# Forgetting attention: adding the two halves of a block's accumulator on GpSimd, one half moved between rows by DMA

## The chip, the cores and the metric

The kernel runs on one core of one Trainium2 chip. The metric is the device time of one execution in microseconds (us). Runs of the same kernel differ by about 0.1%: the kernel before took 2542.85 to 2546.45 us in three runs, with a median of 2545.35 us.

The core has five engines with a queue each: TensorE (PE; its weight loads are listed as PEld), VectorE (DVE), ScalarE (ACT), GpSimd (POOL) and SyncE (SP). Here SyncE only issues transfers for the core's 16 DMA engines. An engine takes its instructions in program order, and one that waits for a semaphore holds those behind it.

## The reference

Two layers of a trunk on 2048 tokens of width 1024, all in float32. Each layer normalizes x, projects it by one weight, mixes tokens in three branches (spatial gating, retention, forgetting attention), gates each branch, and projects the result back. The change lies in the third branch, which has six heads of width 64:

```python
def _forgetting_attention(q, k, v, f_logit):
    scale = d ** -0.5
    cum_f = jnp.cumsum(jax.nn.log_sigmoid(f_logit), axis=1)
    for i in range(s // Q_BLOCK):
        logits = jnp.einsum('bqhd,bkhd->bhqk', qb, kb) * scale
        logits = logits + cum_f[:, :, q0:q1, None] - cum_f[:, :, None, :q1]
        logits = jnp.where(causal, logits, -jnp.inf)
        p = jax.nn.softmax(logits, axis=-1)
        outs.append(jnp.einsum('bhqk,bkhd->bqhd', p, vb))

f_out = f_out.reshape(b, s, F_WIDTH) * jax.nn.silu(f_g)
```

## The kernel before

Each layer runs as three stages on TensorE: the input projection with gating and retention, the attention, and the output projection. Every float32 operand of a matmul is split into a high and a low part (`H`/`L`, `PH`/`PL`), so that a product is a sum of fast matmuls.

**The attention stage** (`fox`) goes over heads 0 to 5, over four blocks `s` of 512 queries each, and over the 4s + 4 key tiles `j` of 128 keys that a block sees: 240 steps a layer. One step has five parts in the order `ORDER = "ltesv"`:

- `t_step` transposes four pieces of exponentials into a bank `T` (L661) and makes the parts `PH` and `PL` of it, three steps ahead of their use. Usually ScalarE makes PH (L673) and VectorE PL (L672). For the key tiles in `ON_POOL` (tile 3 of block 0; 5 of block 1; 4 and 8 of block 2; 4, 8 and 12 of block 3) ScalarE copies T to SBUF (L666) and GpSimd makes both (L667, L668).
- `l_step` issues the VectorE half that the step before put off.
- `e_step` takes exponentials on ScalarE (L648).
- `s_step` computes scores for later blocks, about 19 steps ahead (L614 with the keys' high parts, L615 with the tile `kL`), and VectorE takes their running minimum `mn` (L632).
- `v_step` multiplies with the values into the bank `acc` (L690 with PH, L691 with PL). The values are 128 columns wide, the high parts in the first 64 and the low parts in the last 64, so `acc` holds two halves, one in rows 0 to 63 and one in rows 64 to 127, and the attention output is their sum.

**After each block** a generator, `finish(h, s, acc)`, runs beside the loop; each `bg.tick()` at the end of a step takes it to its next `yield`. A pair of heads (even e = 0, odd e = 1) shares a tile `o2`, one in its upper and one in its lower 64 rows.

- First tick: ScalarE copies the lower half of acc to a tile `lo` (L703).
- Second tick: VectorE adds the halves into o2 (L705) and sums the denominators (L710). For an even head that is all.
- For an odd head VectorE takes the reciprocal (L713) and SyncE loads the gate (L716). Two ticks on TensorE transposes the reciprocals (L719), ScalarE copies them (L721), and SyncE writes 4 KB of them to DRAM (L723). Two ticks on SyncE reads them back, broadcast over 64 rows, twice (L726). Four ticks on GpSimd multiplies gate and reciprocals (L728), one tick on it multiplies o2 with that (L730), and three ticks on SyncE writes the result (L732).

**Loads** of the next head's keys, values and queries go through a list in `FoxLoads`; one entry is issued on SyncE in each step (L569), ahead of `bg.tick()`. After the last key tile of block 0, and behind the tick of that step, `ld.kv(h + 1)` puts three loads on the list (two of 512 KB, one of 1024 KB), for heads 1 to 4; after block 1 `ld.c(h + 1)` puts on the two `kL` loads of the next head.

The order of all this is the program's order; nothing rearranges it. Tiles of tag "u" share 29 slots in turn.

Of the kernel before, what the change touches and what calls it, by code (L numbers as in the profile page):

```python
# [10 lines left out]
F32 = mybir.dt.float32  # L11
F32R = mybir.dt.float32r
AF = mybir.ActivationFunctionType
ALU = mybir.AluOpType
# [4 lines left out]
P = 128  # L19
# [4 lines left out]
HD = 64  # L24
# [13 lines left out]
FX, RA, RB, RC, RD = 2, 2, 4, 1, 3  # L38
# [32 lines left out]
def wait(n):  # L71
    for _ in range(n):
        yield
# [3 lines left out]
def trunk(ctx, tc, a, out):  # L77
    nc = tc.nc
# [8 lines left out]
    up = ctx.enter_context(tc.tile_pool(name="up", bufs=NU))  # L87
# [3 lines left out]
    def U(name, dt=F32):  # L91
        return up.tile([P, 1024], dt, name=name, tag="u")
# [3 lines left out]
    def bank(name, tag):  # L96
        n, bufs = BANKS[tag]
        return ps.tile([P, n], F32, name=name, tag=tag, bufs=bufs)
# [4 lines left out]
    def small(name, shape, bufs=4):  # L103
        return tp.tile(shape, F32, name=name, tag=name, bufs=bufs)
# [466 lines left out]
    class Fox:  # L571
# [124 lines left out]
        def finish(self, h, s, acc):  # L696
            m, e = divmod(h, 2)
            if e == 0 and s % 2 == 0:
                self.o2[s // 2] = U("o2")
            o2 = self.o2[s // 2][:, (s % 2) * 512:(s % 2 + 1) * 512]  # L700
            yield
            lo = up.tile([HD, 512], F32, name="lo", tag="u")
            nc.scalar.copy(out=lo, in_=acc[HD:P, :])  # L703
            yield
            nc.vector.tensor_tensor(out=o2[e * HD:(e + 1) * HD], in0=acc[0:HD, :], in1=lo, op=ALU.add)  # L705
            if e == 0:
                self.rd[s] = small("rd", [P, 2, 4], bufs=6)
            rd = self.rd[s]
            den = self.den.pop((h, s))
            nc.vector.tensor_reduce(out=rd[:, e], in_=den[:, :, 0:s // 2 + 1], op=ALU.add, axis=AX.X)  # L710
            if e == 0:
                return
            nc.vector.reciprocal(out=rd, in_=rd)  # L713
            gy = U("gy")
            g, rb = gy[:, 0:512], gy[:, 512:1024]
            nc.sync.dma_start(out=g, in_=self.gscr[m][:, s * 512:(s + 1) * 512])  # L716
            yield from wait(FX)
            T = bank("rT", "S")
            nc.tensor.transpose(T[0:8, 0:P], rd.rearrange("p e r -> p (e r)"), ident)  # L719
            rT = tp.tile([8, P], F32, name="rT", tag="yr")  # L720
            nc.scalar.activation(out=rT, in_=T[0:8, 0:P], func=AF.Copy, scale=0.5)  # L721
            scr = dram.tile([8, P], F32, name=f"rd{self.ld.l}{m}{s}")
            nc.sync.dma_start(out=scr, in_=rT)  # L723
            yield from wait(RA)
            for i in range(2):
                nc.sync.dma_start(out=rb[i * HD:(i + 1) * HD], in_=scr[4 * i:4 * i + 4].rearrange("r p -> (r p)").partition_broadcast(HD))  # L726
            yield from wait(RB)
            nc.gpsimd.tensor_tensor(out=g, in0=g, in1=rb, op=ALU.mult)  # L728
            yield from wait(RC)
            nc.gpsimd.tensor_tensor(out=rb, in0=o2, in1=g, op=ALU.mult)  # L730
            yield from wait(RD)
            nc.sync.dma_start(out=self.y[s][1][m], in_=rb)  # L732
# [203 lines left out]
    for l in range(depth):  # L936
# [3 lines left out]
        for i in fox(fx):  # L940
            if i >= len(fx.V) - OW and i % OD:
                next(og, None)
            if l == depth - 1 and i == len(fx.V) - OPRE:
                op = out_proj(l, y, W, og, x_src, lambda t: out[t * P:(t + 1) * P, :], None, None, None)
            elif i == len(fx.V) - OPRE:
# [5 lines left out]
                op = out_proj(l, y, W, og, x_src, lambda t, x1=x1: x1[t], hT, (nw, W0), cur)  # L951
# [44 lines left out]
```

## Time and profile before

| | |
|---|---|
| median of 3 runs | 2545.35 us (2542.85 to 2546.45) |
| the profiled execution | 2542.31 us, of which the span of its instructions is 2540.5 us |
| PE busy | 2500.7 us (98%) |
| PEld busy | 2139.5 us (84%) |
| DVE busy | 1658.1 us (65%) |
| ACT busy | 1258.9 us (50%) |
| POOL busy | 865.4 us (34%) |
| DMA | 229.87 MB, 90 GB/s on average, nearly all from SP's queue |

The shares are averages over stages with different limits, so the attention stages (about 800 to 1089 and 2060 to 2349 us) are read by themselves. A row of the timeline gives start and duration in us, the engine, the line, the operation, what it writes and reads, and in brackets how long the engine was idle before it and what released it. "SPq" is SyncE issuing a transfer; the duration is that of the issue, not of the transfer.

### The profile page before, as it was taken

How to read it: one execution, taken by the hardware profiler on the slowest of the kernel's cores; microseconds unless marked ns; L12 is line 12 of the kernel's file. 1: busy time of each engine (PE TensorE's matmuls, PEld its weight loads, DVE VectorE, ACT ScalarE, POOL GpSimd, SP SyncE). 2: the span in 40 equal slices, each digit the busy share in tenths (PEclk: the TensorE clock that was granted, in tenths of full speed). 3: DMA queues.
4: the chain of work that ended last, by engine and by line, in shares of the span. 5: the costliest groups of instructions: out<-in, count | busy, mean ns of one | idle time of the engine just before them, and what ended most of it. 6: DMA issues, size and time to landing. Idle time of an engine off the chain costs nothing. (4 is left out here: it accounts for less than half of the span.)

```text
span 2540.5 us, 39565 instructions
## 1 busy us (share of the span) xinstructions
PE 2500.7 (98%) x13112; PEld 2139.5 (84%) x13112; DVE 1658.1 (65%) x4161; ACT 1258.9 (50%) x2967; POOL 865.4 (34%) x1384
## 2 busy tenths in 40 slices
PE   9999999999999999999999999999999999999998
PEld 8988899887888888878898889997878888887887
DVE  5544477667668999854454445676666689998433
ACT  7634433333335888843344444333333368888222
POOL 3111366444433333331120114664444323244200
PEclk9999999999999999999999999999999999999999
DMA  6335411101041445253432354111010414543443
GB/s 210 119 91 123 109 46 34 41 14 42 10 109 42 100 109 149 72 183 132 138 124 75 99 121 112 29 38 42 14 38 19 103 45 108 123 132 102 156 149 116
DMA packets 187061, 229.87 MB, mean 90 GB/s; under 512 B 23272, under 2 KB 128680, under 8 KB 185320
## 3 DMA queue, kind: packets, MB, share of 16 engines
q1 hardware_dynamic: 186856, 227.34, 31.9%
q8 instruction: 104, 1.70, 0.3%
q14 instruction: 101, 0.83, 0.1%
HBM read 149.20 MB, written 78.09 MB: 89 GB/s over the span
## 5 line engine op out<-in xcount | busy, mean ns | idle before, releaser
L491 PE MATMUL z<-HL 128*128 128x512 f32 (+2 forms) x1536 | 587.4, 382 | 2.4 <-ACT HL L176 2.4
L493 PE MATMUL z<-HL 128*128 128x512 f32 (+2 forms) x1536 | 561.3, 365 | 0.6 <-DVE HL L178 0.4
L492 PE MATMUL z<-HL 128*128 128x512 f32 (+2 forms) x1536 | 560.0, 365 | 1.5 <-POOL HL L178 1.5
L178 DVE TENSOR_TENSOR HL<-hT,HL 128x512 fp32r<-128x512 f32 x576 | 426.1, 789 | 41.7 <-ACT HL L176 33.2
L869 PE MATMUL oo<-HL 128*128 128x512 f32 x1488 | 355.4, 395 | 0.3 <-DVE HL L178 0.2
L178 POOL TENSOR_TENSOR HL<-wf,HL 128x384 fp32r<-128x384 f32 (+2 forms) x162 | 190.7, 1183 | 430.9 <-ACT HL L176 326.5
L176 ACT CAST HL<-hT 128x512 fp32r<-128x512 f32 x576 | 323.8, 626 | 0.0
L869 PEld LDWEIGHTS oo<-HL 128*128 128x128 f32 x1488 | 273.3, 188 | 57.9 <-DVE HL L178 1.2
L493 PEld LDWEIGHTS z<-HL 128*128 128x128 f32 x1536 | 288.8, 188 | 33.9 <-DVE HL L178 2.0
L491 PEld LDWEIGHTS z<-HL 128*128 128x128 f32 x1536 | 290.3, 189 | 24.5 <-ACT HL L176 3.3
L492 PEld LDWEIGHTS z<-HL 128*128 128x128 f32 x1536 | 290.3, 189 | 24.1 <-POOL HL L178 1.9
L672 DVE TENSOR_TENSOR PHL<-T,PHL 128x512 fp32r<-128x512 f32 (+3 forms) x402 | 241.3, 604 | 17.5 <-ACT PHL L673 17.4
L673 ACT CAST PHL<-T 128x512 fp32r<-128x512 f32 (+3 forms) x402 | 206.4, 520 | 56.6 <-PE T L661 41.2
L266 PE MATMUL z<-HL 128*128 128x512 f32 x576 | 224.4, 390 | 0.0
L267 PE MATMUL z<-HL 128*128 128x512 f32 x576 | 224.1, 389 | 0.0
L268 PE MATMUL z<-HL 128*128 128x512 f32 x576 | 224.1, 389 | 0.0
L614 PE MATMUL S<-kv,q 128*128 128x512 f32 (+1 forms) x480 | 211.0, 442 | 2.0 <-DVE mn L632 2.0
L350 ACT COPY v<-z 128x128 f32<-128x128 f32 x96 | 25.6, 267 | 354.0 <-DVE w L346 353.9
L690 PE MATMUL acc<-PHL,kv 128*128 128x512 f32 x480 | 181.0, 377 | 0.0
L691 PE MATMUL acc<-PHL,kv 128*128 128x512 f32 x480 | 176.3, 367 | 0.9 <-DVE PHL L672 0.9
L648 ACT ACTIVATE row<-row,mn 128x1024 f32<-128x1024 f32 (+2 forms) x192 | 158.2, 824 | 35.9 <-DVE mn L632 35.9
L615 PE MATMUL S<-kL,q 66*128 66x512 f32 (+1 forms) x480 | 175.9, 366 | 0.0
(160 smaller groups left out, 4348.6 us busy)
## 6 DMA issues: line engine op xcount, KB each, us to landing
x<-x SPq DMA_DIRECT2D x48, 512.0 KB
qk<-zHL SPq DMA_DIRECT2D x192, 128.0 KB
wf<-w_in SPq DMA_DIRECT2D x96, 192.0 KB
vscr<-vv SPq DMA_DIRECT2D x32, 384.0 KB
wf<-w_in SPq DMA_DIRECT2D x48, 256.0 KB
kv<-qk SPq DMA_DIRECT2D x24, 512.0 KB
kv<-vscr SPq DMA_DIRECT2D x12, 1024.0 KB
q<-qk SPq DMA_DIRECT2D x48, 256.0 KB
```

Of the source, the lines that this page charges most:

```text
L176: nc.scalar.copy(out=v(H), in_=src)
L178: eng.tensor_tensor(out=v(L), in0=src, in1=v(H), op=ALU.subtract)
L266: mm(z, lhsT=wH[:, c], rhs=H, start=(k == 0), stop=False)
L267: mm(z, lhsT=wH[:, c], rhs=L, start=False, stop=False)
L268: mm(z, lhsT=wL[:, c], rhs=H, start=False, stop=(k == KT - 1))
L491: mm(z[:, :n], lhsT=H[:, c], rhs=wH[:, :n], start=(k == 0), stop=False)
L492: mm(z[:, :n], lhsT=H[:, c], rhs=wL[:, :n], start=False, stop=False)
L493: mm(z[:, :n], lhsT=L[:, c], rhs=wH[:, :n], start=False, stop=(k == KT - 1))
L614: mm(S[:, :n], lhsT=Q[0][:, qc], rhs=K[:, kc], start=True, stop=False)
L672: self.low = lambda: nc.vector.tensor_tensor(out=PL[:, c0:], in0=T[:, c0:], in1=PH[:, c0:], op=ALU.subtract)
L673: nc.scalar.copy(out=PH[:, c0:], in_=T[:, c0:])
L869: mm(oo[g], lhsT=x[:, c], rhs=w[g][i], start=(k == 0 and first), stop=(k == KT - 1 and last))
```

## The change

ScalarE copies the whole accumulator, 128 rows, to the left half of a tile `two`. A DMA on SyncE's queue copies the 64 rows that belong to the other head of the pair into the rows of this head, in the right half of the tile. GpSimd adds the two halves into o2, two ticks later than VectorE did before: for an even head behind a wait of FX = 2 ticks, for an odd head behind the issue of L723's DMA.

```diff
-            lo = up.tile([HD, 512], F32, name="lo", tag="u")
-            nc.scalar.copy(out=lo, in_=acc[HD:P, :])
+            two = U("two")
+            mine, other = (slice(e * HD, (e + 1) * HD), slice((1 - e) * HD, (2 - e) * HD))
+            nc.scalar.copy(out=two[:, 0:512], in_=acc)
+            nc.sync.dma_start(out=two[mine, 512:1024], in_=two[other, 0:512])
             yield
-            nc.vector.tensor_tensor(out=o2[e * HD:(e + 1) * HD], in0=acc[0:HD, :], in1=lo, op=ALU.add)
             if e == 0:
                 self.rd[s] = small("rd", [P, 2, 4], bufs=6)
             rd = self.rd[s]
             den = self.den.pop((h, s))
             nc.vector.tensor_reduce(out=rd[:, e], in_=den[:, :, 0:s // 2 + 1], op=ALU.add, axis=AX.X)
             if e == 0:
+                yield from wait(FX)
+                nc.gpsimd.tensor_tensor(out=o2[mine], in0=two[mine, 0:512], in1=two[mine, 512:1024], op=ALU.add)
                 return
...
             nc.sync.dma_start(out=scr, in_=rT)
+            nc.gpsimd.tensor_tensor(out=o2[mine], in0=two[mine, 0:512], in1=two[mine, 512:1024], op=ALU.add)
             yield from wait(RA)
```

## Rows read from the trace of the kernel before

**Rows 1.** Busy us of each engine in the first attention stage, granted clock, DMA.
```profile
800.00:1089.00 289.00, 283.54 (x1748) 239.58 (x1747) 262.84 (x715) 251.76 (x550) 106.57 (x116) 1.00 0.42 110
```
**Rows 2.** Waits of TensorE, whole trace: us in total, times, longest.
```profile
PE T L661 <- DVE PHL L672: 7.1, 15, 1.3
...
PE S L614 <- DVE mn L632: 2.0, 9, 0.2
```
**Rows 3.** Groups by line: count, busy us, mean ns, idle before.
```profile
L705 DVE TENSOR_TENSOR o<-acc,lo 64x512 f32<-64x512 f32 x48 | 32.7, 681 | 0.8
...
L728 POOL TENSOR_TENSOR gy<-gy 128x512 f32<-128x512 f32 x24 | 31.0, 1293 | 59.1 <-DMA gy<-rd 40.1 <-ACT PHL L673 7.0 <-DVE mn L632 5.9
```
**Rows 4.** Timeline of ScalarE at the end of block 0, head 1.
```profile
856.54 0.58 ACT L703 COPY lo<-acc 64x512 f32<-64x512 f32 x1
857.15 1.07 ACT L673 CAST PHL<-T 128x512 fp32r<-128x512 f32 x2
```
**Rows 5.** Timeline of SyncE, GpSimd and TensorE in the same place.
```profile
849.50 0.75 SPq L569 DMA_DIRECT2D q<-qk  x2
850.30 0.45 SPq L569 DMA_DIRECT2D kv<-qk  x1
...
859.44 1.38 SPq L723 DMA_DIRECT2D rd<-rT  x1
864.80 1.09 SPq L726 DMA_DIRECT2D gy<-rd  x2
...
867.09 0.31 SPq L569 DMA_DIRECT2D kL<-qk  x1
...
868.32 1.29 POOL L728 TENSOR_TENSOR gy<-gy 128x512 f32<-128x512 f32 x1 [7.72 <-DMA gy<-rd]
...
870.29 1.29 POOL L668 TENSOR_TENSOR PHL<-Ts,PHL 128x512 fp32r<-128x512 f32 x1
...
871.63 0.19 PEld L691 LDWEIGHTS acc<-PHL,kv 128*128 128x128 f32 x1 [0.23 <-POOL PHL L668]
...
874.74 0.31 PE L614 MATMUL S<-kv,q 128*128 128x128 f32 x1
```
**Rows 6.** Busy us, granted clock, DMA share and GB/s while the loads run.
```profile
850.50:863.10 12.60, 12.33 (x75) 10.02 (x74) 11.81 (x33) 11.33 (x26) 2.29 (x4) 1.00 1.01 218
```
**Rows 7.** DMA issues of the q loads, with KB each.
```profile
q<-qk SPq DMA_DIRECT2D x48, 256.0 KB
...
q<-qk SPq DMA_DIRECT2D x48, 132.0 KB
```
**Rows 8.** Timeline of SyncE where no large load is under way.
```profile
885.79 0.28 SPq L723 DMA_DIRECT2D rd<-rT  x1
887.01 1.09 SPq L726 DMA_DIRECT2D gy<-rd  x2
```
**Rows 9.** Timeline of the fourth such place (block 0, head 3, second layer).
```profile
2207.25 0.45 SPq L569 DMA_DIRECT2D kv<-qk  x1
...
2213.49 0.58 ACT L703 COPY lo<-acc 64x512 f32<-64x512 f32 x1
...
2220.91 1.09 SPq L726 DMA_DIRECT2D gy<-rd  x2
...
2226.02 0.62 POOL L667 TENSOR_SCALAR PHL<-Ts 128x512 fp32r<-128x512 f32 x1 [0.22 <-POOL gy L728]
2226.72 1.30 POOL L668 TENSOR_TENSOR PHL<-Ts,PHL 128x512 fp32r<-128x512 f32 x1
...
2228.43 0.19 PEld L691 LDWEIGHTS acc<-PHL,kv 128*128 128x128 f32 x1
```
**Rows 10.** Busy us by engine and granted clock, at the beginning and the end.
```profile
12.00:18.70 6.70, 5.15 (x17) 4.54 (x18) 5.79 (x5) 4.54 (x11) 6.45 (x7) 0.50 0.80 260
...
2534.00:2537.00 3.00, 0.00 (x0) 0.00 (x0) 1.77 (x3) 0.69 (x2) 0.93 (x3) 1.00 0.00 0
2537.00:2538.00 1.00, 0.00 (x0) 0.00 (x0) 0.34 (x1) 0.00 (x0) 0.00 (x0) 0.89 0.47 174
```

## The prediction

> **What bounds the kernel now.** I read the busy shares by stretch first, then who waits for whom on TensorE, then the queue of SyncE, because the change adds a DMA to it, and last GpSimd's instructions in order of time. The changed code runs only in the two attention stages, about 800 to 1089 us and 2060 to 2349 us. In the first [rows 1] TensorE is busy 283.5 of 289 us, VectorE 262.8 (91%), ScalarE 251.8, GpSimd only 106.6. So TensorE is the bound and VectorE runs close behind it. In the whole trace TensorE waits 7.1 us for VectorE's L672 and 2.0 us for its running minimum [rows 2], so about 9 us is all that less work on VectorE could give back directly.
>
> **VectorE.** The change removes 48 additions (6 heads by 4 blocks by 2 layers) of 681 ns [rows 3]: 48 x 0.681 = 32.7 us of VectorE's busy time. That is no gain by itself, since TensorE sets the pace; it is one only where the addition stands in a chain of VectorE's work that TensorE waits for. Bounds: 0 and the 9.1 us of rows 2. An addition comes once in about 12 us and VectorE has 9% of slack to catch up, so I take a little under half, 4 us gained.
>
> **ScalarE.** The copy now has 128 rows and not 64, both with 512 columns. The old one takes 0.58 us; two casts of 128 x 512 take 1.07 us together [rows 4]. I cost it at nothing; bounds are -0.05 to +0.05 us apiece, 2.4 us in all, and ScalarE is 13% idle [rows 1].
>
> **GpSimd.** 48 additions from SBUF are added. A product of two 128 x 512 operands takes 1293 ns there [rows 3]; a 64-row addition may take the same or half, so 31 to 62 us of work on an engine that is 63% idle. I take 62. Its place is what counts: the addition stands three steps of the loop after the copy, and in blocks 2 and 3, where GpSimd makes high and low parts, the next such instruction after it is at the sixth step (the first one at step 2 is ahead of it). With 1.2 us a step (289 us for 240 steps) that leaves 3.6 us for an addition of 1.3 us. It is covered as long as its DMA has landed; the bound without cover is 48 x 1.3 = 62 us.
>
> **The DMA's own time.** The trace has no transfer between rows of SBUF. The nearest are the two 64-row broadcasts of L726, issued at 864.80 and landed by 868.32 [rows 5]: 3.5 us at most; the 4 KB note of L723 needs 1.2 us on a free queue (885.79 to 887.01 [rows 8]) and 5.4 us behind loads (859.44 to 864.80 [rows 5]). I take 3 us and 0.5 us for its issue. Its data is ready at step 3 then, and the addition doesn't wait much.
>
> **SyncE's queue, where I see the price.** SyncE issues in program order and stands still at an instruction whose semaphore isn't up. In the kernel before, SyncE issues nothing in the finish of an even head's block, and in that of an odd head the first DMA that waits for a computed value is L723, three steps on. So SyncE runs ahead: at the end of block 0 of head 1 (heads count from 0) it issues the first load of keys and values for head 2 at 850.30, though ScalarE's copy of that block ran at 856.54 to 857.12 [rows 4, 5]. In program order the new DMA stands before these loads (tick runs before ld.kv) and waits for the copy. So the new DMA leaves at 857.12, takes 0.45, and the first key load leaves at 857.6: 7.3 us later than now.
>
> What depends on it: the note L723 (reciprocal row to DRAM) is behind the loads in the queue. It was issued at 859.44, and L726, which waits for its landing, went at 864.80. The DMA engines were fully busy (share 1.01, 218 GB/s) from 850.5 to 863.1 [rows 6], so the note waited for the loads to drain. From the first key load to L726 it is 864.80 - 850.30 = 14.5 us. Afterwards the pair of q loads that is ahead of it now (256 + 132 KB [rows 7], 1.8 us at 218 GB/s) has drained before 857, and the new DMA's 128 KB adds 0.6 us: 14.5 - 1.8 + 0.6 = 13.3. So L726 goes at 857.6 + 13.3 = 870.9, 6.1 us later.
>
> GpSimd is held by that. L728 waits for L726's landing (idle 7.72 us before it now) and stands in GpSimd's queue directly before the high and low parts of block 2's fifth key tile (L667, L668). These end at 871.58, and TensorE's L691 already waits 0.23 us for them [rows 5]. With L728 6.1 us later, TensorE stands 6.1 - 0.05 = 6.05 us longer. In the last such place [rows 9] the copy is at 2213.49, the first key load at 2207.25 and L726 at 2220.91; the same sum puts L726 at 2214.5 + 13.66 - 1.2 = 2227.0, 6.1 us later. There GpSimd idles 0.22 us between L728 and L667, and L691 comes 0.41 us after L668, so 5.44 us are left. There are four such places: blocks 0 of heads 1 and 3, in both layers (heads 2 and 4 have loads too, but there SyncE is held at L723 of the odd head before, so nothing ran ahead; head 5 has no loads after it). Four times the mean of 6.05 and 5.44, 5.75: 23.0 us lost. Bounds: 0, if the note gets past the loads, and 4 x 7.3 = 29 us, if all of the delay comes through.
>
> Behind the delayed L726 stand the new DMA of block 1, the low keys (kL) and the next row notes; all of them move with TensorE's stall. kL leaves at 867.09 for a score matmul at 874.74 [rows 5], 7.7 us ahead; afterwards it leaves at about 873.5 for one at 880.6, 7.1 us, and I cost it at nothing. Unshielded it would cost 1 to 2 us in each of eight places.
>
> **The clock.** A stall of almost 6 us may cost TensorE its upper level. At the end of the trace TensorE stops at 2534.0; the clock is still 1.00 (2.4 GHz) to 2537 and 0.89 on average in the next microsecond, so it fell there to 0.5 (1.2 GHz). At the beginning it works for 5.15 us in 12.0 to 18.7 at 0.50 before the level rises [rows 10]. If that is repeated, 6.6 us at half speed cost 3.3 us, for four stalls 13.2. One fall in the trace does not show that a shorter stop is enough each time, so I take half: 6.6 us; bounds 0 and 13.2.
> The Trainium skill, "TensorE: Matmul & The Clock Gate", section "HAM oscillation", describes a kernel that is put back to the lower clock at every wait for a DMA and starts each burst cold. By it all four stalls would pay, and the sum would be 6.6 us higher; no stall inside the loop of this trace is long enough to show it.
>
> **Sum.** 23.0 + 6.6 - 4.0 = +25.6 us. The profiled execution took 2542.3 us (its span is 2540.5), so its like would take 2567.9. It ran 3.0 us below the median of the runs shown, 2545.35; from the median the forecast is 2571 us. Its own range: stalls alone with VectorE's whole 9 us gained, 2545.35 + 23 - 9 = 2559; stalls at 29 with the whole clock, 2545.35 + 29 + 13.2 = 2588.
>
> **Rivals.** (1) Faster: the small note isn't held by the big loads. L723 has 8 rows, so it need not use the engines that drain last; L726 then goes about as now and only VectorE's relief is left: 4 to 9 us gained, 2536 to 2541. It decides wherever the note lands within 1.2 us of its issue as at 885.79 [rows 8]; against it stand the 5.4 us of 859.44 to 864.80.
> The Trainium skill, "DMA: Bandwidth & Descriptors", section "Queues, rings and completion order", says completion within one issuer's queue isn't in order and that a transfer uses only as many engines as divide its rows; by that this rival could come true, and rows 5 speak against it.
> (2) About no change: the loads start late but drain faster or earlier than I count, so that L728 is only 1 to 2 us late: 4 x 1.5 - 4 = +2, 2547 us, to 2553 at most. For it: in the last place 0.63 us of delay would go unnoticed [rows 9]. Against it: 218 GB/s with a share of 1.01 leaves the DMA engines nothing to speed up.
> (3) Slower still: the new DMAs land late elsewhere too, behind the loads of heads 2 and 4, hold GpSimd's addition past the high and low parts behind it, and kL comes late: 8 places x 1 to 2 us on top, 2580 to 2595. Against it: I count about 1 us of slack in each.
>
> **Chances.** Forecast 0.66, rival 1 0.07, rival 2 0.13, rival 3 0.14. A measurement of this kernel can't tell less than 0.2% (5.1 us) from no change: 2540.3 to 2550.4. Faster than that is rival 1, with a little of it inside: with tails 0.07. The same: most of rival 2, 0.10. Slower: forecast, rival 3 and the rest, 0.83. The range runs from 2550 to 2588: it leaves out rival 1, most of rival 2 and the top of rival 3, under 2 in 10.
>
> **What would show it.** Right: in the four places SyncE issues the key loads after the copy, about 7 us later; L726 about 6 us later after it; L728 idles some 13 us for it; and L690 or L691 of block 2, key tile 4, waits about 6 us for GpSimd's L668, four times. A granted clock below 1.00 behind these stalls gives the clock's term. VectorE should be some 33 us less busy, GpSimd 60 us more, and TensorE's waits for L672 a few microseconds shorter. The forecast is wrong if L728 in these places is on time (rival 1), if the stall is under 2 us (rival 2), or if TensorE waits for GpSimd or kL in many more than four places (rival 3).

## The result and the profile after

The changed kernel takes 2576.53 us (median of 4 runs, 2573.97 to 2578.09), the kernel before beside it 2544.34 us. The ratio is 1.0127, with a 95% interval of 1.0115 to 1.0139: some 32 us slower, 5.5 us above the forecast of 2571 and inside its range. The profiled execution took 2575.42 us, with a span of 2573.6.

The busy times of the whole span, the changed kernel:
```profile
PE 2507.5 (97%) x13112; PEld 2146.7 (83%) x13112; DVE 1632.4 (63%) x4113; ACT 1250.0 (49%) x2967; POOL 925.2 (36%) x1432
```
VectorE is busy 25.7 us less than before, GpSimd 59.8 us more. (The 48 additions of 681 ns that VectorE lost are 32.7 us, as forecast; busy time counts overlapping instructions once.) The two attention stages by stretch (columns as in [rows 1]) hold the whole loss:
```profile
799.20:1105.30 306.10, 288.31 (x1748) 243.98 (x1746) 250.31 (x690) 247.26 (x551) 134.36 (x139) 0.97 0.43 113
2077.80:2381.70 303.90, 286.78 (x1748) 243.18 (x1746) 250.40 (x690) 246.91 (x550) 134.94 (x138) 0.97 0.43 114
```
A stage is 15 to 17 us longer than the 289 us of [rows 1], VectorE and GpSimd have slack in it, and the granted clock is 0.97 and not 1.00. Next, what TensorE waits for (us in total, times, longest), against [rows 2]:
```profile
PE acc L690 <- POOL PHL L667: 20.2, 4, 5.5
PE T L661 <- DVE PHL L672: 11.2, 12, 2.4
...
PE S L614 <- DVE mn L632: 0.9, 4, 0.2
```
Four waits for GpSimd's high part hold 20.2 us; before, that row doesn't exist. The first of the four in the order of time, SyncE's queue first, which answers to [rows 5] (line numbers have moved: L723 is L726 now, L726 is L730, L728 is L732; the new DMA is L705):
```profile
855.94 0.47 SPq L705 DMA_DIRECT2D two<-two  x1
856.46 0.59 SPq L569 DMA_DIRECT2D kv<-qk  x1
...
858.92 6.16 SPq L726 DMA_DIRECT2D rd<-rT  x1
868.96 1.09 SPq L730 DMA_DIRECT2D gy<-rd  x2
870.16 0.54 SPq L705 DMA_DIRECT2D two<-two  x1
870.79 0.48 SPq L569 DMA_DIRECT2D kL<-qk  x1
```
then GpSimd, and TensorE's weight loads:
```profile
872.77 1.26 POOL L732 TENSOR_TENSOR gy<-gy 128x512 f32<-128x512 f32 x1 [11.88 <-DMA gy<-rd]
...
874.67 0.19 PEld L690 LDWEIGHTS acc<-PHL,kv 128*128 128x128 f32 x1 [5.21 <-POOL PHL L667]
876.02 0.29 PEld L691 LDWEIGHTS acc<-PHL,kv 128*128 128x128 f32 x1 [1.16 <-POOL PHL L668]
```
This is to be read from the bottom up. A weight load of TensorE waits 5.21 us (the matmul behind it 4.79) for a high part that GpSimd could only make after its product L732; L732 had waited 11.88 us for the broadcast L730, which SyncE could issue only when the 4 KB note L726 had landed, 10.0 us after the note's issue (5.4 before). The note is behind the key and value loads, and those are behind the DMA of the change, which waited for ScalarE's copy at 855.32. The first key load left at 856.46; it was 850.30 before.

The granted clock around these stops (columns as in [rows 10]):
```profile
871.00:873.00 2.00, 0.00 (x0) 0.00 (x0) 0.29 (x1) 0.37 (x2) 0.23 (x1) 1.00 0.71 213
874.70:881.70 7.00, 6.35 (x19) 4.67 (x20) 1.55 (x5) 1.06 (x2) 5.64 (x5) 0.51 0.49 145
977.00:987.30 10.30, 7.06 (x22) 5.39 (x22) 1.98 (x5) 1.11 (x3) 8.67 (x8) 0.51 0.58 172
2151.30:2158.30 7.00, 4.40 (x14) 3.22 (x14) 0.76 (x2) 0.59 (x1) 6.52 (x7) 0.51 0.54 146
2253.70:2264.10 10.40, 6.71 (x20) 5.04 (x21) 1.79 (x5) 1.06 (x2) 7.55 (x8) 0.51 0.54 157
```
The first row is the middle of the stop at 869.9 to 874.7: TensorE does nothing, and the clock is still at 2.4 GHz; there it falls as the stop ends. The other rows are the stretches at 1.2 GHz, 6.8, 10.2, 6.8 and 10.2 us, four times of four. In the second, third and fourth place the level falls while TensorE still stands (the stops end at 979.69, 2153.34 and 2256.83), here in the second:
```profile
977.30:979.60 2.30, 0.00 (x0) 0.00 (x0) 0.00 (x0) 0.00 (x0) 1.81 (x2) 0.50 0.74 224
```
So TensorE works at 1.2 GHz for 6.8, 7.8, 4.9 and 7.2 us.

One more loss was not in my sum: at the end of each stage TensorE comes 2.63 and 2.37 us later at the value products of (5, 3, 7) (head, block, key tile). In the first layer, SyncE, ScalarE and TensorE:
```profile
1089.04 0.48 SPq L705 DMA_DIRECT2D two<-two  x1
1089.69 0.46 SPq L736 DMA_DIRECT2D yT<-gy  x1
...
1090.74 0.40 SPq L773 DMA_DIRECT2D wf<-w_out  x1
```
```profile
1096.49 0.62 ACT L176 CAST HL<-wf 128x512 fp32r<-128x512 f32 x1 [3.11 <-DMA wf<-w_out]
...
1098.37 0.66 PE L661 MATMUL T<-ident,rows 128*128 128x128 f32 x4 [2.41 <-DVE PHL L672]
```
The load of the output projection's weights is issued after the new DMA of block 2. ScalarE, which splits these weights between the casts of the attention, stands at one that has not landed for 3.11 us, the cast L673 behind it comes late, then VectorE's L672, then TensorE. It is the same mechanism with another load, for the greater part: against TensorE's steps this load leaves 1.7 us later than before (1074.45 there) and is another 1.0 us longer under way. The granted clock behind this stop of 2.41 us stays at 1.00:
```profile
1098.40:1101.80 3.40, 2.65 (x17) 2.07 (x18) 2.67 (x5) 2.69 (x6) 2.65 (x4) 1.00 0.89 317
```

### The profile page after: what moved, and what is told of

Read it like the earlier page. It is cut to its first block, busy times and chain, and to the rows that moved or that the text cites. A ratio compares the mean times of both kernels' runs of the same rounds, so it can differ in the third digit from the quotient of the medians.

```text
span 2573.6 us, 39755 instructions
## 1 busy us (share of the span) xinstructions
PE 2507.5 (97%) x13112; PEld 2146.7 (83%) x13112; DVE 1632.4 (63%) x4113; ACT 1250.0 (49%) x2967; POOL 925.2 (36%) x1432
## 5 line engine op out<-in xcount | busy, mean ns | idle before, releaser
L493 PEld LDWEIGHTS z<-HL 128*128 128x128 f32 x1536 | 289.1, 188 | 34.3 <-DVE HL L178 2.4
L672 DVE TENSOR_TENSOR PHL<-T,PHL 128x512 fp32r<-128x512 f32 (+3 forms) x402 | 242.1, 605 | 24.2 <-ACT PHL L673 21.4
L673 ACT CAST PHL<-T 128x512 fp32r<-128x512 f32 (+3 forms) x402 | 207.3, 522 | 69.8 <-PE T L661 50.0
L690 PE MATMUL acc<-PHL,kv 128*128 128x512 f32 x480 | 184.2, 384 | 20.2 <-POOL PHL L667 20.2
L691 PE MATMUL acc<-PHL,kv 128*128 128x512 f32 x480 | 179.6, 374 | 4.0 <-POOL PHL L668 2.5
```

Of the source, the lines that this page charges most:

```text
L493: mm(z[:, :n], lhsT=L[:, c], rhs=wH[:, :n], start=False, stop=(k == KT - 1))
L672: self.low = lambda: nc.vector.tensor_tensor(out=PL[:, c0:], in0=T[:, c0:], in1=PH[:, c0:], op=ALU.subtract)
L673: nc.scalar.copy(out=PH[:, c0:], in_=T[:, c0:])
```

## The experiments

Three theories at the start. S: the time goes where SyncE stands at the new DMA until ScalarE has copied, since loads are queued behind it; neither the DMA's traffic nor GpSimd's work matters. G: it goes to GpSimd, whose 48 additions stand in order before the high and low parts. D: it goes to the bytes that the new DMAs add (48 of 128 KB), which delay the loads. The kernel before took 2545.13 us beside the first four kernels, 2544.75 beside the others. Four expectations were met (e3, e6, e7, e8); e1, e2 and e4 came out 11.5, 4.9 and 3.2 us above the range expected under S, and e5 0.3 us above its range.

**e1_act_queue.** The DMA is issued from ScalarE's queue, after the copy, and no longer from SyncE's.
```
-            nc.sync.dma_start(out=two[mine, 512:1024], in_=two[other, 0:512])
             yield
+            nc.scalar.dma_start(out=two[mine, 512:1024], in_=two[other, 0:512])
```


> The changed kernel, with the DMA between rows issued by ScalarE's queue one tick later instead of by SyncE's. Theory S (SyncE stands at the new DMA and the next head's loads leave about 6 us late): SyncE runs ahead as in the kernel before, the four stalls of about 6 us and the four stretches at half clock go, 2535 to 2550 us; ScalarE pays 48 issues of up to 0.5 us, which may cost up to 10 us of that. Rival G (GpSimd's 48 additions of 1.29 us hold its high and low parts): the additions are all still there, 2570 to 2580. Rival D (the 6.3 MB of extra DMA traffic delays the loads): the traffic is still there, 2570 to 2580.

Measured: 2561.49 us, ratio 1.0062 (1.0046 to 1.0077): 15 of the 32 us come back. In the profiled execution the four long stops and their half clock are gone, as S says. The rest is a new loss: the loads run ahead again, and the DMA of the block before, which leaves after them, lands late. ScalarE's queue, GpSimd and a cast of ScalarE in the first layer:
```profile
851.98 0.48 ACTq L706 DMA_DIRECT2D two<-two  x1
```
```profile
860.44 1.28 POOL L714 TENSOR_TENSOR o<-two 64x512 f32<-64x512 f32 x1 [7.40 <-DMA two<-two]
```
```profile
861.75 0.27 ACT L673 CAST PHL<-T 128x128 fp32r<-128x128 f32 x1 [1.29 <-POOL o L714]
```
Its data was there 8.5 us after the issue; until then the addition of the even head's block (L714) held GpSimd for 7.40 us, and a cast of ScalarE came late behind it. Over the span L714 waits 36.4 us for its DMA, in the changed kernel 14.2. Behind the stages TensorE waits for GpSimd's split of the output weights, 5.7 us where the changed kernel has 0.3; in the first layer an addition of GpSimd ahead of that split (L727) had stood 4.85 us for its DMA:
```profile
PE oo L873 <- POOL HL L178: 5.7, 2, 3.2
```
So with this queue GpSimd's order does matter, though only through the late DMA. The profiled execution (2554.88 us) is the fastest of the four runs, so its trace covers some 10 us of loss and leaves about 6 open. The other three runs have a mean granted clock of 0.996, this one 0.998: some 10 us more at half clock (an estimate from the two means), in places that no trace shows.

**e2_dma_late.** In the last block of an even head and the first of an odd one, SyncE gets the new DMA after the loads (and in the odd head after the note). The additions of these blocks move behind their DMAs, so GpSimd's order changes with SyncE's.
```
+            late = (e, s) in ((0, 3), (1, 0))
+            move = lambda: nc.sync.dma_start(out=two[mine, 512:1024], in_=two[other, 0:512])
...
+            if not late:
+                move()
...
+                if late:
+                    yield from wait(6)
+                    move()
+                    yield from wait(FX)
+                add()
...
+            if late:
+                move()
+            else:
+                add()
...
+            if late:
+                add()
```


> The changed kernel, with only the DMAs of block 3 of even heads and block 0 of odd heads moved behind the next head's loads and behind L726's DMA in SyncE's program order (and their additions moved after them). Theory S: the loads for heads 2 and 4 are free to leave early again, so the four stalls go; 35 us of stall and clock come off, the price at the end of each stage stays: 2538 to 2550. Rivals G and D: as many additions and as many bytes as in the changed kernel, 2570 to 2580.

Measured: 2554.94 us, ratio 1.0039 (1.0025 to 1.0052). 22 of 32 us come back by order alone, with all copies, DMAs and additions still done. The order of SyncE's queue and that of the additions were changed together; e3 tells them apart. As e1 and e2 move the same bytes without the four long stops, D falls. TensorE's four long waits have shrunk:
```profile
PE acc L690 <- POOL PHL L667: 3.4, 3, 2.0
```
In the first layer the value products there still come 2.17 and 1.34 us later, with some half clock behind them, in the second 0.40 and 0.25 us. Step and stretch behind it together, the four places make TensorE 13.3 us later than in the kernel before, 35.5 us in the changed kernel; why the first layer's are larger stays open. The loss at (5, 3, 7) is as large as before (2.62 and 2.33 us), as it should be, since those DMAs had not been moved.

**e3_dma_alone.** The kernel before, its VectorE addition kept, and one more DMA of the same size that waits for ScalarE's copy and goes to a tile that nothing reads. GpSimd adds nothing.
```
+    spare = const.tile([P, 512], F32, name="spare")
...
             nc.scalar.copy(out=lo, in_=acc[HD:P, :])
+            nc.sync.dma_start(out=spare[HD:P], in_=lo)
```


> The kernel before, VectorE's addition untouched, with one DMA more on SyncE in each block that waits for ScalarE's copy and moves its 64 rows to a tile that nobody reads. Theory S: the whole price without VectorE's relief, four stalls of about 6 us, their stretches at half clock and 2 to 3 us at the end of each stage: 2575 to 2592. Rival G: no GpSimd addition, so as before, 2540 to 2550. Rival D: as in theory S; the runs with the DMA on another queue or later tell S and D apart.

Measured: 2581.70 us, ratio 1.0144 (1.0128 to 1.0161): the whole loss without a single GpSimd addition. (It is 36.6 us, as VectorE keeps its addition here.) G falls. The four steps come 4.3 to 4.8 us later (4.95 to 5.64 in the changed kernel), the end of the stages 2.94 and 2.31 us. The same stops, SyncE, then GpSimd, then TensorE's waits (lines below L115 are one higher here):
```profile
856.81 0.47 SPq L705 DMA_DIRECT2D spare<-lo  x1
857.33 0.59 SPq L570 DMA_DIRECT2D kv<-qk  x1
...
869.62 1.37 SPq L728 DMA_DIRECT2D gy<-rd  x2
```
```profile
873.50 1.26 POOL L730 TENSOR_TENSOR gy<-gy 128x512 f32<-128x512 f32 x1 [13.23 <-DMA gy<-rd]
```
```profile
PE acc L691 <- POOL PHL L668: 17.5, 4, 4.6
```

**e4_two_copies.** No DMA: ScalarE copies both halves to the head's rows, 64 rows each, and GpSimd adds them.
```
-            nc.scalar.copy(out=two[:, 0:512], in_=acc)
-            nc.sync.dma_start(out=two[mine, 512:1024], in_=two[other, 0:512])
+            nc.scalar.copy(out=two[mine, 0:512], in_=acc[0:HD, :])
+            nc.scalar.copy(out=two[mine, 512:1024], in_=acc[HD:P, :])
```


> The changed kernel without the DMA: ScalarE copies each 64-row half of the accumulator straight to the rows of this head, two copies of 0.58 us, and GpSimd adds them as in the changed kernel. Theory S: no stalls, no half clock; VectorE's relief of 4 to 9 us is kept and 48 more copies on ScalarE (28 us, in stages where it is 87% busy) take back 0 to 12: 2536 to 2550. Rival G: additions as in the changed kernel, 2570 to 2580. Rival D: no traffic, as theory S.

Measured: 2553.24 us, ratio 1.0033 (1.0020 to 1.0046). No stop is longer than 1.95 us, so the DMA is needed for the four stops. But the kernel is 8 us slower than the one before: a second copy costs as much as the first,
```profile
L705 ACT COPY two<-acc 64x512 f32<-64x512 f32 x48 | 28.0, 583 | 0.6
L704 ACT COPY two<-acc 64x512 f32<-64x512 f32 x48 | 27.6, 575 | 0.5
```
and TensorE's wait for L672, which follows a cast of ScalarE, rises from 7.1 us [rows 2] to 13.3 us in 28 waits. Of the 11 us by which the profiled execution is longer than that of the kernel before, 5.2 lie in the last block of each stage, where a stop of 1.95 us has 3.4 us at half clock behind it, in both layers:
```profile
1082.80:1086.20 3.40, 3.40 (x13) 2.81 (x12) 1.83 (x3) 1.78 (x4) 2.42 (x2) 0.50 0.65 220
```
Ahead of this stop ScalarE works without a gap from the second copy (L705 at 1078.34) to the casts at 1080.58, VectorE waits 1.85 us for one of them and comes to L672 late, and TensorE waits for that; no addition of GpSimd is in this chain. So 28 us more on an engine that is at 87% in these stages cost more than 33 us less on VectorE, at 91%, gave. For the other half of the loss this is argued from the waits for L672.

**e5_busy.** The changed kernel, with work that nothing reads put into the four stops, so that TensorE doesn't stand still.
```
+                    if (h, s, j) in ((1, 2, 4), (3, 2, 4)):
+                        warm = bank("warm", "B")
+                        for _ in range(45):
+                            nc.tensor.transpose(warm[:, 0:P], ident, ident)
```


> The changed kernel with 45 more transposes of a constant on TensorE ahead of the value products of (1, 2, 4) and (3, 2, 4) in both layers, into a bank that nothing reads, so that TensorE works on in the four places where it stands still now. The wait on SyncE is left as it is. Theory S with the clock as a term of its own (after the four stalls the changed kernel runs at a granted 0.50 for 6.8 to 10.2 us each, 34 us in all, and the stage loses about 10 us more by it): the four waits for the key block stay, as transposes in place of idle time, the granted clock stays at 1.00 behind them, and the time is about 2566 us (2563 to 2570). Rival (what is lost behind the stalls is a refilling of the queues of work between the engines, not the clock): the half clock goes, the time stays at 2573 to 2578.

Measured: 2570.27 us, ratio 1.0100 (1.0087 to 1.0114), 6.3 us less than the changed kernel. The first and the third of the stops:
```profile
868.30:875.00 6.70, 6.70 (x57) 6.32 (x55) 2.94 (x7) 3.24 (x6) 2.08 (x3) 1.00 0.54 146
875.00:878.00 3.00, 2.19 (x13) 1.60 (x12) 0.46 (x1) 0.59 (x1) 2.92 (x3) 1.00 0.28 73
...
2152.40:2156.00 3.60, 3.60 (x14) 3.01 (x13) 0.76 (x2) 0.63 (x2) 3.35 (x4) 0.53 0.43 118
```
Where the transposes reach to the end of the wait the clock stays at 1.00 and the place loses 2.74, 2.90 and 2.27 us less (first, second and fourth). In the third place the transposes ended 1.32 us too early, the clock fell for 3.4 us, and the place loses 1.3 us more. The four together make 6.6 us, near the 6.3 measured. Counted behind the stop alone, where the changed kernel has the half clock and this one has not, the difference is 2.63, 2.95 and 2.71 us. In the third place the changed kernel loses 2.83 us behind the stop, 1.2 of which is L691's wait at full clock in the other places here; that leaves 1.6 for the clock, so 9.9 us in four.

**e6_mixed.** The addition of the kernel before in the 9 blocks of a layer behind whose DMA loads are queued, that of the change in the other 15.
```
+            old = h == 5 or (e, s) in ((0, 3), (1, 0))
+            if old:
+                nc.scalar.copy(out=two[0:HD, 0:512], in_=acc[HD:P, :])
+            else:
+                nc.scalar.copy(out=two[:, 0:512], in_=acc)
+                nc.sync.dma_start(out=two[mine, 512:1024], in_=two[other, 0:512])
             yield
+            if old:
+                nc.vector.tensor_tensor(out=o2[mine], in0=acc[0:HD, :], in1=two[0:HD, 0:512], op=ALU.add)
...
+            if not old:
+                nc.gpsimd.tensor_tensor(out=o2[mine], in0=two[mine, 0:512], in1=two[mine, 512:1024], op=ALU.add)
```


> The changed kernel, with the addition of the kernel before (ScalarE copies 64 rows, VectorE adds from PSUM, no DMA) in 9 of the 24 blocks of a layer: the last block of an even head, the first of an odd head, and all four of head 5; the other 15 are added by GpSimd with the DMA. Theory S: no DMA that waits for ScalarE stands ahead of the loads of a key pair or of the output weights any more, so the four stalls, the half clock and the loss at the end of the stage all go (no wait of TensorE above 3 us at these places), and VectorE's relief is left for 15 of 24 blocks, about 4 to 5 of its 7 to 8 us: 2538 to 2543 us, faster than the kernel before. Rival (each DMA that waits costs a little wherever it stands in SyncE's order, about 0.4 us a block): 2546 to 2552 us.

Measured: 2541.42 us (11 runs), ratio 0.9988 (0.9980 to 0.9997): a little faster than both kernels, 3.3 us below the one before. 30 DMAs and 30 GpSimd additions are still there. The queue in the first place is as before the change again, and GpSimd is in time:
```profile
849.55 0.47 SPq L569 DMA_DIRECT2D kv<-qk  x1
...
863.36 1.09 SPq L739 DMA_DIRECT2D gy<-rd  x2
```
```profile
867.08 1.29 POOL L741 TENSOR_TENSOR gy<-gy 128x512 f32<-128x512 f32 x1 [7.23 <-DMA gy<-rd]
```
In three of the four places no more than 0.2 us is lost; at (1, 2, 4) of the second layer this execution still comes 1.9 us later. The rival, a price for each DMA that waits, falls: 30 such DMAs are left and the kernel is faster.

**e7_end_kept.** The same edit with the old addition in head 5 alone.
```
+            old = h == 5
```


> The changed kernel, with the addition of the kernel before in the four blocks of head 5 alone, where the loads of the output weights come behind the DMA on SyncE. Theory S: the loss of 2.4 to 2.6 us at the end of each stage (the wait of the value products of (5, 3, 7)) goes, the four stalls and their half clock stay: 5 us off, 2570 to 2573 us. Rival (the end of the stage is late because ScalarE and GpSimd carry more there, not because of the loads): the loss at (5, 3, 7) stays above 2 us in each layer, 2574 to 2578 us.

Measured: 2572.31 us, ratio 1.0109 (1.0095 to 1.0122). The steps at (5, 3, 7) are no later than those before them any more, in either layer, and TensorE's waits for L672 are down from 11.2 us:
```profile
PE T L661 <- DVE PHL L672: 5.9, 8, 1.3
```
4.2 us less in the medians, whose intervals overlap by a little; the trace of the place is what decides. The edit takes the wide copies and GpSimd's additions out of head 5 as well, so alone it doesn't tell the queue from them. e3 does: there ScalarE and GpSimd do in head 5 what they did before, only the DMA is added, and the same step comes 2.94 and 2.31 us later.

**e8_relief.** The kernel before without its addition: ScalarE copies the upper half of the accumulator straight to the output, and the lower half's share of the sum is left out. There is no new DMA and no GpSimd addition.
```
-            lo = up.tile([HD, 512], F32, name="lo", tag="u")
-            nc.scalar.copy(out=lo, in_=acc[HD:P, :])
+            mine, other = (slice(e * HD, (e + 1) * HD), slice((1 - e) * HD, (2 - e) * HD))
+            nc.scalar.copy(out=o2[mine], in_=acc[0:HD, :])
...
-            nc.vector.tensor_tensor(out=o2[e * HD:(e + 1) * HD], in0=acc[0:HD, :], in1=lo, op=ALU.add)
```


> The kernel before with its addition left out altogether: ScalarE copies the upper 64 rows of the accumulator straight to the head's rows (as many rows and columns as it copied before), VectorE adds nothing, GpSimd adds nothing, no DMA is added; the lower half of the sum is missing from the output. It measures VectorE's relief alone, some 680 ns in 48 blocks. My term for it was -4 us (bounds 0 to 9.1); the changed kernel's trace between its stalls suggests 7 to 8 us: 2537 to 2539 us. Rival (VectorE has slack in most blocks and the gains read between the stalls are only time that the stalls had pushed there): 2543 to 2546 us.

Measured: 2538.56 us (9 runs), ratio 0.9977 (0.9967 to 0.9986): VectorE's relief is worth 6.2 us, by the interval 3.6 to 8.4. TensorE's weight loads wait less often for VectorE (before: 15 and 12 times, 9.6 and 4.9 us):
```profile
PEld T L661 <- DVE PHL L672: 8.5, 8, 1.8
...
PEld S L614 <- DVE mn L632: 2.4, 6, 0.5
```
By step, the whole gain lies at the first four steps of block 1, in all six heads and both layers: 0.4 to 0.7 us each, 7.4 us in all in the profiled execution, and 0.4 us are lost at all other steps together. The changed kernel gains 8.2 us at the same steps. So VectorE's additions stood in TensorE's way only there, behind the short block 0; which of them it was, that of block 0 or that of the block before it, the steps don't show.

## Why the prediction was right, and where its sizes were off

Direction, place and mechanism were right. That the time came out within 5.5 us is in part luck: two losses were taken too small (by 2.6 and 3.3 us) and one of 5.0 us was missing, and a relief that was 2.2 us larger than forecast made up for some of it; and the forecast started from a median of three runs that was 1.0 us above that of the runs beside the changed kernel. What each term of the sum measured, in us; "by trace" is how much later TensorE's value products come at that step than before:

| term | predicted | measured | from |
|---|---|---|---|
| VectorE's relief | -4.0 (0 to 9.1) | -6.2 | e8 |
| four stops | +23.0 (0 to 29) | +25.6 | by trace: 4.95 + 5.64 + 5.09 + 5.10 for L690, and 4 x 1.2 for L691 (1.10 to 1.23 in e5 where the clock stayed full) |
| the clock | +6.6 (0 to 13.2) | +9.9 | by trace, against e5: 2.63 + 2.95 + 1.6 + 2.71 |
| end of the stage | 0 | +5.0 | by trace: 2.63 + 2.37; e7 |
| low key loads, ScalarE, GpSimd | 0 | about 0 | by trace: -0.1 at all other steps together; e3, e6 |
| sum | +25.6 | +34.3 | profiled executions: +33.1 |

The 1.2 us between the sum and the traces are less than the relief's own interval.

**SyncE's queue.** Each link came as forecast. The first key load left 6.2 us later in absolute time, but the copy itself came 1.2 us earlier than before (855.32, 856.54 in [rows 4]), so 7.4 us against it (7.3 forecast). From the first key load to the broadcast 12.5 us passed (13.3 forecast). TensorE was 1.7 us ahead of the kernel before at the first stop, 0.46 us of which stood at the first step of the stage, before any changed code. L732 came 4.45 us later, 6.2 against TensorE's steps. I had TensorE wait at L691; it is L690 that waits, because L667 too stands behind L732, and L691 waits again for L668: 6.15 to 6.84 us a place together, where I had 5.44 to 6.05. In the fourth place I subtracted 0.63 us of slack that did not turn up.

**The clock.** I took half of 3.3 us a stop, because one fall doesn't show that a shorter stop is enough each time. It was enough each time, at 1.6 to 3.0 us apiece, which is half-way between my term and its bound. The Trainium skill, "TensorE: Matmul & The Clock Gate", section "HAM oscillation", describes a kernel that is put back at each wait for data and starts each burst cold. The trace agrees for the four stops, with 0.51 behind four of four, and e5 shows that it is the standing still that does it; it does not agree for the stops of 2.41 and 2.15 us at the ends of the stages, behind which the clock stays at 1.00.

**The step that was missing** is the end of the stage. Under "the price" I asked which loads stand behind the new DMA, and stopped at the keys: "head 5 has no loads after it". It has none of keys, but out_weights issues the weights of the output projection in the same stretch. Rival 3 had the kind of it (loads late elsewhere), not the place. The step that was missing is worth 5.0 us.

**VectorE.** The size was low and its source not shown: the waits of [rows 2] shrink by 1.5 us in e8, and the same waits in the list of the weight loads, which I had not read, by 3.6; but TensorE's waits at L691 grow by 2.0 us at the same time, so the lists of waits don't account for the 6.2 us. The steps do (e8): the gain is at the beginning of block 1 alone. I had spread it over all 48 blocks. Why the addition is in the way only there stays open.

**The rivals.** Rival 1 (the note gets past the loads) needed it to land 1.2 us after its issue; in the four places the broadcast that waits for it went 9.7 to 10.6 us after. The Trainium skill, "DMA: Bandwidth & Descriptors", section "Queues, rings and completion order", lets a later transfer complete before an earlier one; by these 9.7 to 10.6 us the note gained nothing from that here. Rival 2 fell with the waits of 5 us. Rival 3's sign, waits in many more than four places, did not come: TensorE's row for L667 has the four alone. What of the loss of e1 its trace doesn't show stays open, as does what is left in e2 in the first layer.

## What to carry to other kernels

Before a DMA that waits for a computed value is put into a queue that otherwise only prefetches, list everything that is issued behind it up to the next such wait, not only in the function at hand, and ask how far that queue ran ahead: that lead, less the slack behind it, is what is lost. Price a long stop of TensorE with the half clock behind it, here 1.6 to 3.0 us apiece. Where such a DMA is wanted, use it only where nothing is queued behind it (e6), and expect an own queue to have its own price, since the DMA then lands behind the loads (e1).

## What the runs showed of the hardware that was not expected

- Issuing a transfer took 6.16 us (L726 at 858.92, 4 KB; 5.75 to 6.66 in the four places), where [rows 8] have 0.28 us and [rows 5] 1.38: behind loads that have just been issued, the issue itself stretches.
- GpSimd's addition takes the same for 64 rows as its product for 128:
```profile
L727 POOL TENSOR_TENSOR o<-two 64x512 f32<-64x512 f32 x24 | 30.8, 1285 | 11.4 <-DMA two<-two 9.5 <-DVE HL L178 0.7
...
L734 POOL TENSOR_TENSOR gy<-o,gy 128x512 f32<-128x512 f32 x24 | 30.9, 1286 | 0.9
```
- ScalarE's copy of 128 rows takes what one of 64 takes (581 ns against 583 and 575 in e4), so here widening the copy was free and splitting it wasn't:
```profile
L704 ACT COPY two<-acc 128x512 f32<-128x512 f32 x48 | 27.9, 581 | 0.0
```
- The half clock of the four stops lasted 6.8 us in two places and 10.2 us in two. In three of them it began 1.9 to 3.0 us before TensorE's next matmul, so part of it fell on time that was lost anyway.
- The length of a stop alone did not tell whether the clock falls: it stayed at 1.00 behind 2.41 and 2.15 us in the changed kernel, and fell to 0.50 behind 2.58 us at the same step in e5 and behind 1.95 us in e4:
```profile
1094.30:1097.60 3.30, 3.30 (x14) 2.70 (x13) 2.58 (x5) 2.41 (x5) 2.86 (x2) 0.50 0.96 352
```
